# A two-layer decoder trunk with three token mixers: the matmuls of the mixers pinned to the program's order, with new tables for that order

## The chip, the cores and the metric

The kernel runs on one core of one Trainium2 chip. Its time is the time of one execution in microseconds on the device (us). "Before" is the kernel without the change, "after" is the kernel with it. TensorE is called PE in the profile, VectorE is DVE, ScalarE is ACT.

## The reference

The program computes two layers on 256 tokens of width 1024, in float32. Each layer is a half-step feed-forward network, a stage of three token mixers that run on one combined projection of x, a second half-step network, and an input embedding. The mixer stage is what the change touches.

```python
def token_mixing(x, w_in, ...):
    h = (x @ w_in).astype(jnp.float32)
    h_rw, h_gla, h_gdn, h_gate = _split(h, GROUP_SPLITS)
    o_rw = rwkv7_time_mix(h_rw, ...)
    o_gla = gla_mix(*_split(h_gla, GLA_SPLITS), ...)
    o_gdn = gated_deltanet_mix(*_split(h_gdn, GDN_SPLITS), ...)
    branches = jnp.stack([o_rw, o_gla, o_gdn], axis=2)
    proj = jnp.einsum('btnc,ncd->btnd', branches, w_branch)
    gates = jax.nn.sigmoid(h_gate).reshape(B, T, N_BRANCH, D_MODEL)
    merged = jnp.sum(gates * proj, axis=2)
    return merged.astype(x.dtype) @ w_o
```

Each mixer is a recurrence over time that the kernel computes in chunks: RWKV-7 with eight heads of 64, gated linear attention (GLA) with four heads, and gated DeltaNet (GDN) with four heads and a short causal convolution over its q, k and v.

## The kernel before

Every weight is split into a high and a low part so that a float32 product is three matmuls (x high by w high, x low by w high, x high by w low). A weight half arrives by DMA as `raw` (128x1024), ACT casts it to `hi`, and DVE subtracts to get `lo`. `ahead` issues this for the weights to come (four raw buffers, four pairs of hi and lo), and `unit` hands the next block out. PSUM is divided into three sets of banks: A with four, F with two and G with two; the table TAGS says which tile takes which set.

The mixer stage of a layer begins with the block fwa of the projection and ends with the output projection wo of `merge`. Four generators run in it. S (`stream`) computes the projection in blocks: a block `cb` is 48 matmuls of 128x256 into one bank (`col_block`), followed by what takes it out of the bank: `shift_mix` for RWKV (one ACT and one DVE instruction for each half; the tile is called c0, c512, ...), `conv` for GDN (one ACT and three DVE instructions for each half; c3888, c3376), a sigmoid-free copy `sg` to DRAM for the merge gates (`put`), or a copy. Later S projects the finished branches with `project` (tile `pj`). R (`rwkv`), D (`gdn`) and L (`gla`) are the chains of the three mixers. MIX lists the blocks in S's order, ORDER is a string that says which generator takes the next step, from one `yield` to the next.

Names that come up: in RWKV `pw` are the low-rank products of decay and `av`, `l2` the norm of kk (its operand `sq`, its row in the profile called l), `ls`, `bk` operands that are spread out for the Gram matrices `gram`, whose inverse is built in `rig`, `rigt`, `riab` (15 pairs of a multiply and a reduction on DVE), then `rix`, `rih`, and a recurrence of `rp`, `ru`, `rd`, `ry` over chunks; `bh`, `bl` are the high and low parts of the finished branch. In GDN `ab`, `gcol`, `grow`, `dd` are the decays, `un` the unit norms (operand `usq`), `gix`, `gih` the inverse, `gv`, `gd`, `go` the recurrence. In GLA `gk` is the forget gate, `lxb` its logarithm and running sum, `lw` the weighted q and k of a level, `lg` the Gram matrix of a level, `latt` the assembled attention.

A scheduler decides the order of each engine's instructions from the program's order, priorities and its own estimates; between instructions that depend on each other it adds semaphore waits. Each engine then runs its own list from front to back. Where `hold` is set, an instruction made through `Engine.__getattr__` is pinned, so that it keeps its place in the program's order on its engine. Before, only the Gram matmuls of RWKV are held so within the mixers.

Of the kernel before, what the change touches and what calls it, by code (L numbers as in the profile page):

```python
# [19 lines left out]
F32 = mybir.dt.float32  # L20
# [6 lines left out]
TAGS = {"ab": "A", "gcol": "A", "gih": "G", "gks": "G", "ktr": "F", "lc": "F", "lo": "A", "misc": "G", "pa": "G", "pg": "G", "pj0": "A", "pj1": "A", "pq": "A", "pw": "G", "rih": "G", "st0": "A", "st1": "G", "un": "F"}  # L27
# [3 lines left out]
P = 128  # L31
# [181 lines left out]
class Engine:  # L213


    def __init__(self, trunk, engine):
        self.trunk, self.engine = trunk, engine

    def __getattr__(self, name):
        f = getattr(self.engine, name)  # L220

        def call(*args, **kw):
            ins = f(*args, **kw)  # L223
            return self.trunk.pin(ins) if self.trunk.hold else ins

        return call


class Engines:
    def __init__(self, trunk, nc):  # L230
        self.tensor, self.vector, self.scalar = (Engine(trunk, e) for e in (nc.tensor, nc.vector, nc.scalar))
        self.gpsimd, self.sync = nc.gpsimd, nc.sync


class Trunk:
# [112 lines left out]
    def unit(self, *key):  # L348

        assert self.plan[self.used] == key, (self.plan[self.used], key)  # L350
        self.used += 1
        self.subtract()
        n = 1 if key[0] == "fmisc" else 2
        self.ahead(n - len(self.ready))
        parts = [self.ready.pop(0) for _ in range(n)]

        def part(a, n):
            q, o = divmod(a, 1024)
            return parts[q][0][:, o:o + n], parts[q][1][:, o:o + n]

        return part
# [308 lines left out]
    def mixers(self, i):  # L670

        self.got, self.branch, self.over = {}, {}, set()
        self.maker = {"b0": "R", "b1": "L", "b2": "D"}
        self.threads = {"S": self.stream(i), "R": self.rwkv(i), "D": self.gdn(i), "L": self.gla(i)}
        for name in ORDER + "RDLS":
            self.step(name)
        for name in "RDLS":
            while name not in self.over:
                self.step(name)

    def stream(self, i):
# [3 lines left out]
        ps = self.col_block(self.unit("fwa", i))  # L685
# [12 lines left out]
        ab = self.pt.tile([P, NT, 8], F32, tag="ab", name="ab", bufs=1)  # L698
        ps = self.ps("ab", "G")
        for t in range(NT):  # L700
            nc.tensor.transpose(ps[:, 8 * t:8 * t + 8], mx[64:72, t * P:t * P + P], self.ident[64:72, 64:72])
        A.copy(ab[:, :, 0:4], ps[:, :16].rearrange("p (t c) -> p t c", c=8)[:, :, 0:4])
        A.activation(ab[:, :, 4:8], ps[:, :16].rearrange("p (t c) -> p t c", c=8)[:, :, 4:8], AF.Sigmoid)
# [185 lines left out]
    def rwkv(self, i):  # L889
# [36 lines left out]
        A.activation(sq, kk, AF.Square)  # L926
        for q in range(2):
# [52 lines left out]
        for q in range(2):  # L980
            for c in range(2):
                m = slice(4 * c, 4 * c + 4)
                pss = [self.ps("gram").rearrange("p (n c) -> p n c", c=P) for _ in range(2)]
                self.hold = True
# [3 lines left out]
                self.hold = False  # L988
# [101 lines left out]
    def rwkv_out(self, t, y, bv, gl):  # L1090
# [4 lines left out]
        A.activation(rs, y, AF.Square)  # L1095
        ps = self.ps("rv")
# [53 lines left out]
    def unit_norms(self, xs):  # L1150
# [17 lines left out]
    def gdn(self, i):  # L1168
# [11 lines left out]
        ab = self.got["misc"][1]  # L1180
# [23 lines left out]
        pg = self.ps("gcol", "G")  # L1204
# [10 lines left out]
        for t in range(NT):  # L1215
            grow = self.ps("grow", "G").rearrange("p (h c) -> p h c", c=P)
# [14 lines left out]
        self.unit_norms([(k, 1.0), (q, float(P) ** -0.5)])  # L1231
# [7 lines left out]
        for t in range(NT):  # L1239
            pk, pq = self.ps("pk", "G"), self.ps("pq", "G")  # L1240
# [53 lines left out]
        for t in range(NT):  # L1294
# [12 lines left out]
            yield  # L1307
            if not t:
                vd = h3(self.s2("gvd"))
                V.tensor_tensor(out=vd, in0=vn, in1=self.head_bc(ec, P), op=ALU.mult)  # L1310
                pd = h3(self.ps("gd"))
# [3 lines left out]
                yield  # L1315
# [10 lines left out]
    def gla(self, i):  # L1326
# [83 lines left out]
        V.tensor_tensor(out=w4[:, :, 2:4], in0=w4[:, :, 2:4], in1=q4[:, :, 2:4], op=ALU.mult)  # L1410
        cross = self.s4("lcross").rearrange("p (a c) -> p a c", c=P)
# [24 lines left out]
    def project(self, i, b, h):  # L1436
# [39 lines left out]
        half(0)  # L1476
        half(1)
# [186 lines left out]
```

## Time and profile before

| | us |
|---|---|
| median of 3 runs | 1574.25 (1574.13 to 1577.86) |
| the profiled execution | 1568.71 |
| its span in the trace | 1566.9 |
| mean granted clock of TensorE | 0.981 |
| mixers of layer 0 | 217.0 to 539.5 |
| mixers of layer 1 | 995.7 to 1318.1 |

The page gives the busy time of every engine, the groups of instructions by line and tile, and the chain of work that ended last. The operations are recorded in a helper, so all of them have one line (L223 before, L224 after), and the groups are told apart by their tiles. A wait of an engine is put down to the instruction that released it. The granted clock is the share of full speed that TensorE was allowed.

### The profile page before, as it was taken

Reading aid. Unit: us, or ns where it says so; the run is one execution under the profiler, and the core shown is the slowest. Engines: PE = TensorE matmul, PEld = TensorE weight load, DVE = VectorE, ACT = ScalarE, POOL = GpSimd, SP = SyncE. Lnnn points to the kernel's source line nnn. Section 1 sums busy time; section 2 is a strip of 40 time slices with the busy share of each in tenths; the row PEclk is TensorE's granted clock in tenths of the full one; section 3 lists DMA queues with packets and bytes.
Section 4 is the critical chain, followed back from the end, with each engine's and each line's share of the span. In section 5 each row is a group of like instructions: output and inputs, shape, how many; then the busy total and the mean of one; then the engine's idle time right before and its main releaser. Section 6 shows DMA issues by size and latency. Waiting matters only on the chain. (4 is left out here: it accounts for less than half of the span.)

```text
span 1566.9 us, 27601 instructions
## 1 busy us (share of the span) xinstructions
PE 1494.9 (95%) x11280; PEld 1356.7 (87%) x11280; DVE 1058.5 (68%) x1597; ACT 873.3 (56%) x1229; POOL 49.1 (3%) x85
## 2 busy tenths in 40 slices
PE   8999999988998999999999999998989889999997
PEld 7999889887987989998789997897979879899986
DVE  5555757787975875556865557577789658745567
ACT  5544558856654554445654445587665555644453
POOL 0000000000002000000000000000000020000001
PEclk9999999989999999999999999999999999999999
DMA  7765655532424655656555666554425256656562
GB/s 257 264 215 189 216 190 161 169 127 80 151 84 168 233 184 177 223 189 216 177 180 192 216 189 194 195 170 153 136 75 156 82 200 219 188 170 222 189 217 81
DMA packets 79775, 277.96 MB, mean 177 GB/s; under 512 B 9376, under 2 KB 9760, under 8 KB 79648
## 3 DMA queue, kind: packets, MB, share of 16 engines
q1 hardware_dynamic: 75744, 262.76, 51.8%
q0 software_dynamic: 3616, 13.11, 2.2%
q8 instruction: 88, 1.44, 0.4%
q10 hardware_dynamic: 288, 0.33, 0.1%
q14 instruction: 39, 0.32, 0.1%
HBM read 264.63 MB, written 11.53 MB: 176 GB/s over the span
## 5 line engine op out<-in xcount | busy, mean ns | idle before, releaser
L223 DVE TENSOR_TENSOR lo<-raw,hi 128x1024 fp32r<-128x1024 f32 (+1 forms) x459 | 555.4, 1220 | 316.1 <-ACT hi L223 313.7
L223 ACT CAST hi<-raw 128x1024 fp32r<-128x1024 f32 (+1 forms) x459 | 474.9, 1047 | 430.1 <-PE h L223 144.1
L223 PE MATMUL h<-xh,hi 128*128 128x256 f32 x1088 | 306.2, 282 | 5.9 <-ACT hi L223 5.5
L223 PE MATMUL h<-xl,hi 128*128 128x256 f32 x1088 | 305.8, 281 | 0.8 <-DVE xl L223 0.8
L223 PE MATMUL h<-xh,lo 128*128 128x256 f32 x1088 | 305.4, 281 | 0.0
L223 PE MATMUL cb<-xh,hi 128*128 128x256 f32 x864 | 247.1, 286 | 14.4 <-DVE c L223 11.1
L223 PE MATMUL cb<-xl,hi 128*128 128x256 f32 x864 | 244.5, 283 | 0.0
L223 PE MATMUL cb<-xh,lo 128*128 128x256 f32 x864 | 243.4, 282 | 0.0
L223 PEld LDWEIGHTS h<-xh,hi 128*128 128x128 f32 x1088 | 204.9, 189 | 7.3 <-ACT hi L223 5.5
L223 PEld LDWEIGHTS h<-xh,lo 128*128 128x128 f32 x1088 | 208.6, 192 | 0.1
L223 PEld LDWEIGHTS h<-xl,hi 128*128 128x128 f32 x1088 | 205.1, 189 | 2.2 <-DVE xl L223 1.0
L223 PEld LDWEIGHTS cb<-xh,hi 128*128 128x128 f32 x864 | 164.7, 191 | 18.8 <-DVE c L223 11.3
L223 PEld LDWEIGHTS cb<-xl,hi 128*128 128x128 f32 x864 | 164.8, 191 | 2.4 <-issue 1.0
L223 PEld LDWEIGHTS cb<-xh,lo 128*128 128x128 f32 x864 | 164.7, 191 | 1.9 <-issue 1.0
L223 PE MATMUL y<-hi,gh 128*128 128x512 f32 x352 | 137.8, 391 | 0.0
L223 PE MATMUL y<-lo,gh 128*128 128x512 f32 x352 | 137.1, 389 | 0.0
L223 PE MATMUL y<-hi,gl 128*128 128x512 f32 x352 | 136.2, 390 | 0.3 <-DVE gl L223 0.3
L223 PE MATMUL tb<-hi,xl 128*128 128x512 f32 x224 | 87.6, 391 | 2.1 <-DVE xl L223 2.1
L223 PE MATMUL tb<-hi,xh 128*128 128x512 f32 x224 | 88.5, 395 | 0.0
L223 PE MATMUL tb<-lo,xh 128*128 128x512 f32 x224 | 88.0, 393 | 0.0
L223 PEld LDWEIGHTS y<-hi,gl 128*128 128x128 f32 x352 | 66.1, 188 | 14.7 <-DVE gl L223 0.8
L223 PEld LDWEIGHTS y<-lo,gh 128*128 128x128 f32 x352 | 66.1, 188 | 12.2
(354 smaller groups left out, 2264.0 us busy)
## 6 DMA issues: line engine op xcount, KB each, us to landing
raw<-in_ws_dram SPq DMA_DIRECT2D x457, 512.0 KB, 4.4
gb<-in_ln_dram SPq DMA_DIRECT2D x16, 512.0 KB, 6.1
gd<-sg SPq DMA_DIRECT2D x32, 256.0 KB, 4.2
sgate<-gd POOLq DMA_DIRECT2D x12, 512.0 KB, 5.8
xd<-x POOLq DMA_DIRECT2D x4, 512.0 KB, 5.8
x<-xd POOLq DMA_DIRECT2D x4, 512.0 KB, 9.0
sw<-in_sw_dram SPq DMA_DIRECT2D x2, 768.0 KB, 8.7
xt<-in_xt_dram SPq DMA_DIRECT2D x4, 256.0 KB, 5.4
```

The costliest lines, as they stand in the source:

```text
L223: ins = f(*args, **kw)
```

## The change

In the mixers PE's instructions are pinned to the program's order, by a flag `eager` that holds for `tensor` alone; DVE and ACT are still ordered by the scheduler. So that the program's order is one to follow, a block yields after its first 24 matmuls, and the chains get further yields so that one step holds one burst of matmuls; the Gram matmuls of a GLA level are issued a step later than their operands; the transposes of `ab` go from the stream to `gdn`. MIX, ORDER and TAGS are new. `unit` asks for two more weight halves ahead while `eager` is set. The work is the same: the same matmuls, DVE and ACT instructions, except for four more ACT_TABLE_LOADs in the whole program.

```diff
-TAGS = {"ab": "A", "gcol": "A", "gih": "G", "gks": "G", "ktr": "F", "lc": "F", "lo": "A", "misc": "G", "pa": "G", "pg": "G", "pj0": "A", "pj1": "A", "pq": "A", "pw": "G", "rih": "G", "st0": "A", "st1": "G", "un": "F"}
+TAGS = {"gk": "G", "lc": "G", "lg": "G", "lo": "G", "misc": "F", "pg": "G", "pj0": "F", "pj1": "F", "st0": "F", "st1": "F",
+        "tp": "G"}
...
-MIX = (C_R, C_K, C_DK, C_LV, (0, 0), C_V, C_LQ, (0, 1), C_DQ, (2, 0), (1, 1), C_DV, (2, 1), (1, 0), ("w", 0, 0),
...
+MIX = (C_K, C_R, (2, 0), C_LQ, (2, 1), C_DK, C_DQ, (1, 0), C_V, C_LV, (1, 1), C_DV, ("w", 1, 0), ("w", 1, 1), (0, 0), (0, 1),
+       ("w", 0, 0), ("w", 0, 1), ("w", 2, 0), ("w", 2, 1))
+ORDER = ("SSSRRSRDLSSDSRSSRSRSRSRSRSSRSRSRSSLSRSLSRSLSRLSRSRLSRSRLSRSRSRDSSSRSRSRDLSSRRSRDLRSRDLRSDLSRDLRS"
...
-            return self.trunk.pin(ins) if self.trunk.hold else ins
+            return self.trunk.pin(ins) if self.trunk.hold or self.first and self.trunk.eager else ins
...
-        self.tensor, self.vector, self.scalar = (Engine(trunk, e) for e in (nc.tensor, nc.vector, nc.scalar))
+        self.tensor, self.vector, self.scalar = (
+            Engine(trunk, e, e is nc.tensor) for e in (nc.tensor, nc.vector, nc.scalar))
...
+        if self.eager:
+            self.ahead(2 - len(self.ready))
...
-    def tok_unit(self, pss, unit, k0, start, stop, x=None):
+    def tok_unit(self, pss, unit, k0, start, stop, x=None, qs=range(2)):
...
             for k in range(8):
                 self.col_mm(ps[:, c * T:c * T + T], unit, k, c)
+            if not c:
+                yield
         return ps
...
+        self.eager = True
         for name in ORDER + "RDLS":
...
+        self.eager = False
...
         A.activation(sq, kk, AF.Square)
+        yield
         for q in range(2):
             ps = self.ps("l2")
...
-                self.hold = True
                 for n in range(4):
                     for e, (r, o) in enumerate(halves):
                         self.mm(pss[e][:, n], bk[q][r, 4 * c + n], ls[e][q][r, 4 * c + n])
-                self.hold = False
...
+        mx = self.got["misc"][1]
+        ab = self.pt.tile([P, NT, 8], F32, tag="ab", name="ab", bufs=1)
+        ps = self.ps("ab")
...
         for n, s in enumerate(LEVELS):
+            if n:
+                grams(*last)
...
-            grams(w, w, 1 + n, s)
+            last = w, w, 1 + n, s
             yield
+        grams(*last)
+        yield
         grams(k, q, 0, 0)
-        yield
```

Three places show how the lists of ACT and DVE come out. The first is ACT's list at the start of layer 0's mixers, where `ab` (GDN's decays) and `lxb` (GLA's gate, taken out of the bank gk) are made. Before, from the end of the tile misc:

```order
L223 COPY gl_2286<-mx 16x256
L223 CAST hi<-raw 128x1024 x2
L223 ACTIVATE c_2494<-cb,om 128x256
L223 COPY ab<-ab 128x2x4
L223 ACTIVATE ab<-ab 128x2x4
L223 ACTIVATE c_2494<-cb,om 128x256
L223 ACT_TABLE_LOAD
L223 ACTIVATE e<-e 128x8
L223 CAST hi<-raw 128x1024 x2
```

and, a hundred rows later, gk's turn:

```order
L223 CAST hi<-raw 128x1024 x2
L223 ACTIVATE sg<-cb 128x512
L223 ACTIVATE c_2363<-c_2363,cv 128x256 x2
L223 ACTIVATE lxb<-gk,cv 128x256 x2
L223 COPY uz<-ru 64x256 x2
```

After, from the copies out of pw on:

```order
L224 ACTIVATE sg<-pw,cv 128x256
L224 ACTIVATE av<-pw,cv 128x256
L224 ACT_TABLE_LOAD
L224 ACTIVATE sg<-sg 128x1024
L224 COPY ab<-ab 128x2x4
L224 ACT_TABLE_LOAD
L224 ACTIVATE ab<-ab 128x2x4
L224 ACTIVATE lxb<-gk,cv 128x256
L224 ACT_TABLE_LOAD
L224 ACTIVATE e<-e 128x8
L224 ACTIVATE lxb<-gk,cv 128x256
L224 CAST hi<-raw 128x1024
```

`ab` and both `lxb` copies now follow directly on pw, with three table loads between them. The second is ACT's list from the spread operands `ls` of RWKV to the copy of a merge gate's block (`sg`) out of its bank. Before:

```order
L223 COPY ls01_2960<-sg_2296 64x8x64
L223 COPY ls11_2962<-sg_2296 64x8x64
L223 ACT_TABLE_LOAD
L223 ACTIVATE c3888_2651<-c3888_2651 128x1024
L223 CAST hi_3089<-raw_3087 128x1024
L223 COPY lv_2891<-st1_2818 128x512
L223 ACT_TABLE_LOAD
L223 ACTIVATE sq_2722<-cs_2357 128x1024
L223 CAST hi_3148<-raw_3146 128x1024
L223 ACTIVATE cs_2357<-cs_2357 128x1024
L223 CAST hi_3154<-raw_3152 128x1024
L223 ACTIVATE sg_2956<-cb_2907 128x512
```

After:

```order
L224 COPY ls10_2773<-sg_2345 64x8x64
L224 COPY ls01_2772<-sg_2345 64x8x64
L224 COPY ls11_2774<-sg_2345 64x8x64
L224 CAST hi_2736<-raw_2734 128x1024
L224 CAST hi_2742<-raw_2740 128x1024
L224 ACTIVATE c0_2583<-cb_2667,om_783 128x256
L224 ACTIVATE sq_2577<-cs_2401 128x1024
L224 CAST hi_2816<-raw_2814 128x1024
L224 ACTIVATE cs_2401<-cs_2401 128x1024
L224 ACTIVATE c0_2583<-cb_2667,om_783 128x256
L224 CAST hi_2822<-raw_2820 128x1024
L224 ACTIVATE sg_2802<-cb_2746 128x512
```

The copy `sg` of block cb_2746 stands behind the rest of the chain (its steps on `sq` and `av` are just ahead of the rows shown), the ls copies and four casts; PE's next block, cb_2826, waits for it. The third is DVE's list at the convolution of the GDN key (c3888). Before, the DVE steps on block cb_2664 stand in a run, and the Gram steps follow some 30 rows later:

```order
L223 TENSOR_TENSOR lo_2822<-raw_2819,hi_2821 128x1024
L223 TENSOR_TENSOR lo_2828<-raw_2825,hi_2827 128x1024
L223 SCALAR_TENSOR_TENSOR c3888_2651<-cb_2664,cv_775,c3888_2651 128x255
L223 SCALAR_TENSOR_TENSOR c3888_2651<-cb_2664,cv_775,c3888_2651 128x254
L223 SCALAR_TENSOR_TENSOR c3888_2651<-cb_2664,cv_775,c3888_2651 128x253
L223 SCALAR_TENSOR_TENSOR c3888_2651<-cb_2664,cv_775,c3888_2651 128x255
L223 SCALAR_TENSOR_TENSOR c3888_2651<-cb_2664,cv_775,c3888_2651 128x254
L223 TENSOR_TENSOR lo_2858<-raw_2855,hi_2857 128x1024
L223 SCALAR_TENSOR_TENSOR c3888_2651<-cb_2664,cv_775,c3888_2651 128x253
L223 TENSOR_TENSOR lo_2864<-raw_2861,hi_2863 128x1024
```

After, a stretch of the steps on blocks cb_3247 and cb_3377:

```order
L224 SCALAR_TENSOR_TENSOR c3888_3234<-cb_3247,cv_775,c3888_3234 128x254
L224 COPY_PREDICATED latt_3013<-masks_79,lg_3406 128x32x8
L224 COPY_PREDICATED latt_3013<-masks_79,lg_3407 128x32x8
L224 STREAM_TRANSPOSE rigt_3553<-rig_3457 128x512
L224 SCALAR_TENSOR_TENSOR c3888_3234<-cb_3247,cv_775,c3888_3234 128x253
L224 TENSOR_TENSOR lo_3466<-raw_3463,hi_3465 128x1024
L224 TENSOR_TENSOR riab_3555<-rigt_3553 128x256
L224 TENSOR_TENSOR lo_3472<-raw_3469,hi_3471 128x1024
L224 SCALAR_TENSOR_TENSOR c3888_3234<-cb_3377,cv_775,c3888_3234 128x255
L224 SCALAR_TENSOR_TENSOR c3888_3234<-cb_3247,cv_775,c3888_3234 128x255
L224 TENSOR_TENSOR rigt_3553<-riab_3555 128x1
L224 SCALAR_TENSOR_TENSOR c3888_3234<-cb_3377,cv_775,c3888_3234 128x254
```

The steps that empty these two banks are spread among the Gram steps, the GLA levels, the transposes and the first steps of the inverse.

More of the change, by code (lines that the diff above doesn't have):

```diff
@@ L54 @@
     0, 128, 256, 384, 512, 544, 672, 800, 802, 804, 932)
-MIX = (C_R, C_K, C_DK, C_LV, (0, 0), C_V, C_LQ, (0, 1), C_DQ, (2, 0), (1, 1), C_DV, (2, 1), (1, 0), ("w", 0, 0),
-       ("w", 1, 1), ("w", 0, 1), ("w", 1, 0), ("w", 2, 0), ("w", 2, 1))
-ORDER = ("RRSRSSSDSSRSRRSSSRRRRRRRRRRSSRSRRRSDRRRRRSRSRDRRRRRRRRDRDSDRLDRRDRDLRDDSDSSSLDLDRLRDRRRDRDDRRRDLRLDD"
-         "SDDDDSDLLSDDDLLRDLSDLLRRLLDSSDSDSLLSSSSDSLDS")
+MIX = (C_K, C_R, (2, 0), C_LQ, (2, 1), C_DK, C_DQ, (1, 0), C_V, C_LV, (1, 1), C_DV, ("w", 1, 0), ("w", 1, 1), (0, 0), (0, 1),
+       ("w", 0, 0), ("w", 0, 1), ("w", 2, 0), ("w", 2, 1))
+ORDER = ("SSSRRSRDLSSDSRSSRSRSRSRSRSSRSRSRSSLSRSLSRSLSRLSRSRLSRSRLSRSRSRDSSSRSRSRDLSSRRSRDLRSRDLRSDLSRDLRS"
+         "DSDLLSRDLRSDLLLSRDLSRDSRDLSRDSRDRSRDSRDSRDRRSRDSRDRRSDSRSRDRSRDDSRDSRDDSRDSRDRDSDSDSSSS")
 LEVELS = (64, 32, 16, 8, 4, 2, 1)
@@ L213, with __init__ @@
 class Engine:
-    def __init__(self, trunk, engine):
-        self.trunk, self.engine = trunk, engine
+    def __init__(self, trunk, engine, first):
+        self.trunk, self.engine, self.first = trunk, engine, first
     def __getattr__(self, name):
@@ L366, in mm3 @@
         self.mm(out, ll, rh, False, stop)
-    def tok_unit(self, pss, unit, k0, start, stop, x=None):
+    def tok_unit(self, pss, unit, k0, start, stop, x=None, qs=range(2)):
         xh, xl = x or (self.xh, self.xl)
-        for q in range(2):
+        for q in qs:
             for t in range(NT):
@@ L679, in mixers @@
                 self.step(name)
+        self.eager = False
     def stream(self, i):
@@ L684, in stream @@
         A = nc.scalar
-        ps = self.col_block(self.unit("fwa", i))
+        ps = yield from self.col_block(self.unit("fwa", i))
         wa = self.pt.tile([P, T], F32, tag="wa", name="wa", bufs=1)
@@ L697, in stream @@
         self.shift_mix(mx, ps[:, :T], 14)
[L698 to L703, printed above, removed]
         nc.gpsimd.memset(gl[:, 1:], 0.0)
@@ L706, in stream @@
         A.copy(gl[32:48, 2], mx[32:48])
-        self.got["misc"] = gl, ab
+        self.got["misc"] = gl, mx
         yield
@@ L711, in stream @@
                 yield "b%d" % item[1]
-                self.project(i, *item[1:])
+                yield from self.project(i, *item[1:])
                 if item != MIX[-1]:
@@ L717, in stream @@
                 for u in range(2):
-                    ps = self.col_block(self.unit("fcol", i, C_MG + item[0] * D + item[1] * 512 + 256 * u))
+                    ps = yield from self.col_block(self.unit("fcol", i, C_MG + item[0] * D + item[1] * 512 + 256 * u))
                     self.put(ps, d, u, AF.Copy)
@@ L725, in stream @@
                 for u in range(2):
-                    self.tok_unit(pss, self.unit("tok", i, item, u), 4 * u, u == 0, u == 1)
-                    if u == 0:
-                        yield
+                    un = self.unit("tok", i, item, u)
+                    for q in range(2):
+                        self.tok_unit(pss, un, 4 * u, u == 0, u == 1, qs=(q,))
+                        if (u, q) != (1, 1):
+                            yield
                 vt = self.s4("lv").rearrange("p (t c) -> p t c", t=2)
@@ L736, in stream @@
                 q, k = qk[:, :512], qk[:, 512:]
-                A.activation(q, self.col_block(self.unit("fcol", i, C_LQ)), AF.Identity, scale=0.125)
+                ps = yield from self.col_block(self.unit("fcol", i, C_LQ))
+                A.activation(q, ps, AF.Identity, scale=0.125)
                 yield
-                A.copy(k, self.col_block(self.unit("fcol", i, C_LK)))
+                ps = yield from self.col_block(self.unit("fcol", i, C_LK))
+                A.copy(k, ps)
                 self.got[item] = q, k
@@ L744, in stream @@
                 for u in range(2):
-                    ps = self.col_block(self.unit("fcol", i, item + 256 * u))
+                    ps = yield from self.col_block(self.unit("fcol", i, item + 256 * u))
                     for c in range(2):
@@ L1095, in rwkv_out @@
         A.activation(rs, y, AF.Square)
+        yield
         ps = self.ps("rv")
@@ L1157, in unit_norms @@
             sqs.append(sq)
+        yield
         for sq in sqs:
             for q in range(2):
-                ps = self.ps("un", "G")
+                ps = self.ps("un")
                 s = slice(q * 512, q * 512 + 512)
@@ L1179, in gdn @@
         yield "misc"
-        ab = self.got["misc"][1]
+        mx = self.got["misc"][1]
+        ab = self.pt.tile([P, NT, 8], F32, tag="ab", name="ab", bufs=1)
+        ps = self.ps("ab")
+        for t in range(NT):
+            nc.tensor.transpose(ps[:, 8 * t:8 * t + 8], mx[64:72, t * P:t * P + P], self.ident[64:72, 64:72])
+        A.copy(ab[:, :, 0:4], ps[:, :16].rearrange("p (t c) -> p t c", c=8)[:, :, 0:4])
+        A.activation(ab[:, :, 4:8], ps[:, :16].rearrange("p (t c) -> p t c", c=8)[:, :, 4:8], AF.Sigmoid)
         e, s, s2, q, x = (small(n) for n in ("e", "s", "s2", "q", "x"))
@@ L1203, in gdn @@
         tri = kc[:, K_INCL:K_INCL + P]
-        pg = self.ps("gcol", "G")
+        pg = self.ps("gcol")
         self.mm(pg[:, :8], tri, x.rearrange("p t h -> p (t h)"))
@@ L1215, in gdn @@
         for t in range(NT):
-            grow = self.ps("grow", "G").rearrange("p (h c) -> p h c", c=P)
+            grow = self.ps("grow").rearrange("p (h c) -> p h c", c=P)
             for h in range(4):
@@ L1230, in gdn @@
         k, q = self.got[C_DK], self.got[C_DQ]
-        self.unit_norms([(k, 1.0), (q, float(P) ** -0.5)])
+        yield from self.unit_norms([(k, 1.0), (q, float(P) ** -0.5)])
         yield
@@ L1239, in gdn @@
         for t in range(NT):
-            pk, pq = self.ps("pk", "G"), self.ps("pq", "G")
+            pk, pq = self.ps("pk"), self.ps("pq")
             for h in range(4):
@@ L1310, in gdn @@
                 V.tensor_tensor(out=vd, in0=vn, in1=self.head_bc(ec, P), op=ALU.mult)
+            yield
+            if not t:
                 pd = h3(self.ps("gd"))
@@ L1314, in gdn @@
                 A.copy(st, pd)
-                yield
             ops = self.ps("go")
@@ L1374, in grams @@
                     "p (a b s) -> p a b s", a=4, s=out.shape[3]))
-        lw = None
+        lw = last = None
         for n, s in enumerate(LEVELS):
+            if n:
+                grams(*last)
             v5 = lambda ap: ap.rearrange("p (m f s) -> p m f s", f=2, s=s)
@@ L1392, in gla @@
             V.tensor_tensor(out=v5(w)[:, :, 1], in0=v5(w)[:, :, 1], in1=v5(q)[:, :, 1], op=ALU.mult)
-            grams(w, w, 1 + n, s)
+            last = w, w, 1 + n, s
             yield
+        grams(*last)
+        yield
         grams(k, q, 0, 0)
-        yield
         w = lw[:, 512:]
@@ L1410, in gla @@
         V.tensor_tensor(out=w4[:, :, 2:4], in0=w4[:, :, 2:4], in1=q4[:, :, 2:4], op=ALU.mult)
+        yield
         cross = self.s4("lcross").rearrange("p (a c) -> p a c", c=P)
@@ L1476, in project @@
         half(0)
+        yield
         half(1)
```

1 line of the change is left out of this document (removed).

## The prediction

> **What bounds the kernel now.** I read the page's first part, then the windows of the two mixer stages, the table of what TensorE (PE) waits for there, and last the clock.
>
> ```profile
> PE 1494.9 (95%) x11280; PEld 1356.7 (87%) x11280; DVE 1058.5 (68%) x1597; ACT 873.3 (56%) x1229; POOL 49.1 (3%) x85
> 217.00:539.50 322.50, 299.17 (x2842) 276.52 (x2841) 242.50 (x435) 208.19 (x304) 13.58 (x25) 0.95 0.45 147
> 995.70:1318.10 322.40, 296.79 (x2841) 274.40 (x2840) 241.90 (x434) 207.65 (x304) 12.72 (x23) 0.96 0.45 148
> ```
>
> The kernel is PE's: 95% busy. The windows run from the first cb matmul of a layer's mixers to its first wo matmul, and are the only stages that the change touches. The columns are length, then busy time of PE, weight loads, DVE, ACT, POOL, then the granted clock. PE idles 322.50 - 299.17 = 23.3 us in layer 0 and 322.40 - 296.79 = 25.6 us in layer 1. Those 49 us, and the clock of 0.95, are all that a better order can win. They are few waits (the first five of layer 0, and the one row of layer 1 that differs most):
>
> ```profile
> PE pj L223 <- ACT bh L223: 6.0, 1, 6.0
> PE cb L223 <- DVE c L223: 5.4, 1, 5.4
> PE un L223 <- ACT usq L223: 4.0, 1, 4.0
> PE gtf L223 <- ACT gt L223: 1.9, 1, 1.9
> PE bkt L223 <- DVE ls L223: 1.3, 1, 1.3
> PE cb L223 <- ACT hi L223: 1.6, 1, 1.6
> ```
>
> The clock falls behind such waits, here after the pair c and usq and after a broken stretch at 437:
>
> ```profile
> 312.50:322.70 10.20, 4.68 (x21) 4.59 (x22) 9.49 (x29) 1.18 (x3) 0.00 (x0) 0.50 0.13 45
> 437.00:442.20 5.20, 2.43 (x30) 1.74 (x26) 2.05 (x5) 4.97 (x7) 0.00 (x0) 1.00 0.00 0
> 442.20:449.00 6.80, 6.12 (x92) 5.43 (x92) 5.66 (x14) 4.24 (x10) 0.00 (x0) 0.50 0.01 2
> ```
>
> At half clock half of the busy time is loss: 4.68 / 2 = 2.3 us and 6.12 / 2 = 3.1 us, 2.7 us in the mean. Each mixer stage has four such stretches (about 10.8 us).
>
> **What the change does, and the durations for it.** The same matmuls, casts and vector operations run before and after. Nothing is removed; only their order, the PSUM banks and, with four more table loads in the program (4 x 1.28 = 5 us of ACT time), ACT's switching differ. So the sum is one of waits: PE's list is now fixed, and at each point I add up what the ACT and DVE lists put ahead of the result that PE wants, and take off the matmuls that PE has to do meanwhile. Mean ns of one, from the groups of layer 0's mixers:
>
> ```profile
> L223 ACT CAST hi<-raw 128x1024 fp32r<-128x1024 f32 x72 | 74.4, 1049 | 58.9 <-PE cb L223 37.4 <-PE pj L223 14.9 <-issue 4.7
> L223 ACT ACT_TABLE_LOAD x21 | 26.9, 1283 | 1.2 <-DVE c L223 0.8
> L223 ACT ACTIVATE sg<-cb 128x512 f32<-128x512 f32 x12 | 7.1, 592 | 0.0
> L223 ACT ACTIVATE c<-cb,om 128x256 f32<-128x256 f32 x12 | 5.5, 474 | 4.0 <-DVE c L223 3.9
> L223 ACT COPY ls<-sg 64x512 f32<-64x512 f32 x4 | 2.5, 620 | 0.0
> L223 ACT ACTIVATE sq<-av,om,cv 128x256 f32<-128x256 f32 x4 | 2.2, 593 | 0.0
> L223 ACT ACTIVATE dd<-grow,gcol 128x128 f32<-128x128 f32 x8 | 2.2, 392 | 0.0
> L223 ACT ACTIVATE sq<-l,eps 128x512 f32<-128x512 f32 x2 | 1.4, 688 | 0.5 <-PE l L223 0.5
> L223 ACT ACTIVATE sg<-sg 128x1024 f32<-128x1024 f32 x1 | 1.1, 1062 | 0.0
> L223 DVE TENSOR_TENSOR lo<-raw,hi 128x1024 fp32r<-128x1024 f32 x73 | 88.3, 1220 | 23.6 <-ACT hi L223 22.6 <-PE cb L223 0.3
> L223 DVE SCALAR_TENSOR_TENSOR c<-cb,cv,c 128x255 f32<-128x255 f32 (+2 forms) x48 | 22.7, 477 | 2.5 <-ACT c L223 1.9
> L223 DVE COPY_PREDICATED latt<-masks,lg 128x256 f32<-128x256 uint8 (+1 forms) x16 | 7.9, 553 | 2.2 <-PE lg L223 2.2
> L223 DVE TENSOR_TENSOR lw<-lw,lqk 128x256 f32<-128x256 f32 x16 | 6.1, 421 | 0.0
> L223 DVE TENSOR_TENSOR ls<-gram,kc 64x512 f32<-64x512 f32 x8 | 5.5, 688 | 0.1
> L223 DVE TENSOR_TENSOR rig<-gram,kc 32x256 f32<-32x256 f32 x8 | 4.7, 590 | 0.1
> L223 DVE TENSOR_TENSOR rigt<-riab 128x1 f32<-128x1 f32 (+14 forms) x15 | 4.6, 306 | 0.5
> L223 DVE TENSOR_REDUCE riab<-rigt 128x1 f32<-128x1 f32 (+14 forms) x15 | 3.6, 238 | 0.4
> L223 DVE STREAM_TRANSPOSE rigt<-rig 128x512 f32<-128x512 f32 x3 | 2.1, 705 | 1.6 <-ACT rit L223 1.6
> L223 DVE TENSOR_TENSOR rig<-riab,kc 128x512 f32<-128x512 f32 x2 | 1.7, 868 | 0.0
> L223 DVE SCALAR_TENSOR_TENSOR q<-q,s 128x8 f32<-128x8 f32 x8 | 1.3, 161 | 0.1
> ```
>
> PE's own pace is the distance of two starts in the timeline; 77 matmuls of cb lie from the first row to the last:
>
> ```profile
> 246.99 0.28 PE L223 MATMUL cb<-xl,hi 128*128 128x256 f32 x1
> 255.73 0.28 PE L223 MATMUL cb<-xh,hi 128*128 128x256 f32 x1
> ```
>
> (255.73 - 246.99) / 77 = 0.1135 us, so a half block of 24 gives 2.7 us of cover and a block of 48 gives 5.45 us. Where a shape has no row of its own here I use the row of the same width.
>
> **The sum for one layer**, in PE's new order. Each term is a wait of PE, with its ends:
>
> 1. pw behind misc. PE has nothing between them: cast (1.05), mx and two wz copies at 0.47 = 2.5. Taken 2.5 (0 to 2.5).
> 2. gk's second bank. The lists have ab and gk right behind pw: table load 1.28, sg 1.06, two tiny ab copies 0.3, table load 1.28, lxb 0.47 = 4.4. Taken 4.0 (2.1, if the first load and half the sg lie earlier, to 4.4).
> 3. gcol. On DVE two lo 2.44, two c 0.95, two 512-wide and two 256-wide lxb steps at 0.69 = 2.8, 16 tiny steps at 0.161 = 2.6: 8.8; one ACT table load and exponential among them 1.4; less 48 cb and gk, 5.7: 4.5. Taken 4.5 (2 to 6).
> 4. l2 wants sq. Behind grow ACT has dd 8 x 0.39, a table load, four hi 4.2, six 256-wide steps 2.8, one 512-wide 0.7, two 1024-wide 2.1 = 14.2; cover 72 cb and grow, 9.2; the first dd run beside grow. Taken 4.6 (3 to 5.1).
> 5. cb behind the first gate block. Its bank is freed by sg, in front of which ACT now has three c 1.4, two table loads 2.6, two sq<-l 1.4, three 1024-wide 3.2, four sq<-av 2.4, four ls 2.5, four hi 4.2; with sg 0.6 that is 18.3. Cover l2 and 96 cb, 11.8: 6.5. A kk step of DVE (1.2) may add to it. Taken 6.5 (5.7 to 7.6).
> 6. The k half of lqk waits for the next sg: four bk and ls pairs at 0.62, two hi, sg: 7.6 - 5.5 = 2.1 (0 to 2.1).
> 7. The convolutions. Their banks are freed by DVE, 12 c steps for C_DK (5.7) and nine of C_DQ (4.3). Before, these stood ahead of the grams; now they stand among and behind seven lo 8.6, eight lw 3.4, six gram and ls steps 2.6, four rig 2.4, four latt 1.7 (these at their narrower 0.43), three transposes 2.1, the whole inverse 15 x 0.306 + 15 x 0.238 = 8.2, and two 0.87 rig: 40.7 in all. PE has 19.3 of its own from there to cb of the third block. 40.7 - 19.3 = 21.4 as upper end; 14.6 if what DVE does before the first grams lies beside earlier waits. Taken 18, as two waits.
> 8. pj of branch R behind bh. The chain rsq, ro, tp, bh is as it was: 6.0 (to 8.9 with two more half-width steps in the queue).
> 9. The rest: the smaller waits of the tables (about 4) remain, and lc, rd, ktr and sgate each meet one of about 1. Taken 8 (4 to 17).
>
> Sum: 2.5 + 4.0 + 4.5 + 4.6 + 6.5 + 2.1 + 18 + 6.0 + 8 = 56.2 us (37 to 75). Old c, un and gtf waits are thereby counted as gone. Added idle: 56.2 - 23.3 = 32.9 and 56.2 - 25.6 = 30.6, together 63.5 us. Clock: seven waits of 4 us or more stand in place of four slow stretches, 3 x 2.7 x 2 = 16.2. The profiled execution's 1568.7 becomes 1648.4. The median lies 1574.25 - 1568.7 = 5.5 above that execution, so **1654 us**.
>
> The slow stretch at 442.20 followed a window in which PE was idle more than half of the time, in pieces. By the Trainium skill ("TensorE: Matmul & The Clock Gate", "Why this matters for your kernels") only gaps of more than about 3 us drop the clock; terms 1 and 6 then cost no clock. By this trace's row they could cost a stretch each, another 2 x 2 x 2.7 = 11 us. I leave them out of the sum either way.
>
> **Rivals.**
> - *DVE has run ahead.* PE's waits 2 to 6 (21.7 us) give DVE time to empty its list, and term 7 shrinks to 5, with one slow stretch less: 1654 - 2 x (13 + 2.7) = 1623; with terms 1 to 3 at their lower ends 1600. For it: DVE idles 80 us of the stage (322.5 - 242.5). Against it: the grams, inverse and conv steps of term 7 all need banks that PE fills only there. Case 1580 to 1620.
> - *The late bursts wait too.* Some 25 short bursts of the chains (ru, rp, ry, rd, gv, go and so on) stand pinned between half blocks, each with 2.7 us of cover for one round of ACT and DVE. If each is 1 us late: 1654 + 2 x 25 = 1704. For it: nothing can now pass a late burst. Against: late in the stage DVE has the lightest load. Case 1690 to 1730.
> - *Faster.* Chains start early and the late waits of before go, while the early ones stay small. With terms 1 to 6 at 8 (only ACT's surplus of work over PE's), term 7 at 5, bh 6, rest 4, idle is 23 us, as now, and only two slow stretches remain: 1574.25 - 0.3 - 2.6 - 4 x 2.7 = 1560.5. It decides at idle and clock loss together under 23.3 + 10.8 = 34 us a layer. Against: the row of sg stands behind 18 us of ACT work in its own list, and PE may not pass it.
> - *Nothing.* The pin has no effect, or every added wait is paid by one that goes: 1574. The order of PE does change, so little is left for it.
>
> **How the numbers follow.** Forecast case (1620 to 1690) 0.51, mild (1580 to 1620) 0.20, heavy (1690 to 1730) 0.14, faster 0.11, nothing 0.04. The range 1582 to 1712 leaves out faster, nothing and the end of heavy, about 0.2. Differences within 0.3%, 4.7 us, can't be told from no change; so faster 0.11, same 0.04, slower 0.85.
>
> **What would show it.** Mixer windows some 40 us longer each at 0.90 to 0.93 clock, all else unmoved. In the table of waits: gcol from DVE near 4.5, l2 from ACT sq near 4.6, cb from ACT sg near 8 to 9, cb from DVE c near 18, un and gtf gone. I am wrong if PE's idle stays under 34 us a layer, if cb from c is under 8, or if the bulk of waits stands in the second half of a mixer stage.

## The result: 1635.0 us, 3.8% slower

The changed kernel takes 1635.0 us in the median of four runs (1634.42 to 1635.29), the kernel before 1574.19 in the runs beside it; the ratio is 1.0384 (95% interval 1.0368 to 1.0399). The profiled execution took 1634.8 us. Its windows over the two mixer stages, cut at the same matmuls as before, from the first cb to the first wo (length, busy PE, weight loads, DVE, ACT, POOL, clock):

```profile
218.70:569.10 350.40, 301.48 (x2841) 279.92 (x2840) 241.35 (x434) 210.17 (x304) 12.85 (x24) 0.93 0.42 135
1031.10:1381.60 350.50, 300.68 (x2841) 279.23 (x2840) 241.73 (x434) 210.12 (x304) 11.99 (x22) 0.93 0.41 135
```

Each stage is 28 us longer than before (322.5 and 322.4). DVE and ACT do the same work in it as before; PE's idle time rose from 23.3 to 350.40 - 301.48 = 48.9 us and from 25.6 to 49.8 us. The rest of the program went from 217.0 + 456.2 + 248.9 = 922.1 us to 932.3. That execution of before was 5.5 us under its own median, and two other kernels whose code outside the mixers is that of before (e2_pin_only and e13_cv_a, below) take 1723.0 - 398.2 - 397.0 = 927.8 and 1572.0 - 322.8 - 321.4 = 927.8 us there. So some 6 of the 10 us are likely the one short execution of before; the others, among them waits of 1 to 2 us at gT and wo, weren't followed further.

Where the 48.9 us lie is shown by the table of PE's waits in layer 0's mixers (us in total, times, longest; its first nine rows):

```profile
PE cb L224 <- ACT c L224: 8.8, 1, 8.8
PE pj L224 <- ACT bh L224: 7.7, 1, 7.7
PE cb L224 <- DVE c L224: 6.3, 1, 6.3
PE cb L224 <- ACT sg L224: 4.7, 1, 4.7
PE l L224 <- ACT sq L224: 3.6, 1, 3.6
PE gcol L224 <- issue: 3.4, 1, 3.4
PE gk L224 <- ACT lxb L224: 3.3, 1, 3.3
PE pw L224 <- issue: 2.7, 1, 2.7
PE rd L224 <- DVE vs L224: 2.6, 3, 1.5
```

These are the places that the prediction named, nearly one for one. The old waits for c behind the grams, at un and at gtf are gone. Where the profile shows no semaphore for a wait it says issue; in layer 1 gcol's stands under DVE x (3.3 us), as forecast. Otherwise layer 1 has the same list within 0.6 us of each, with ACT's ritt (5.7) in the place of DVE's c, and one wait of 1.3 us for hi more. What stands behind such a wait can be read in the timeline of ACT ahead of sg, the copy that frees a bank of the gate block (start, duration, what, and in brackets the idle time before it):

```profile
270.89 1.28 ACT L224 ACT_TABLE_LOAD   x1
272.19 1.27 ACT L224 ACTIVATE sq<-l,eps 128x512 f32<-128x512 f32 x2
273.47 1.28 ACT L224 ACT_TABLE_LOAD   x1
274.76 1.06 ACT L224 ACTIVATE sq<-sq 128x1024 f32<-128x1024 f32 x1
277.12 2.08 ACT L224 ACTIVATE sq<-av,om,cv 128x256 f32<-128x256 f32 x4 [1.29 <-DVE kk L224]
279.11 2.51 ACT L224 COPY ls<-sg 64x512 f32<-64x512 f32 x4
281.64 2.00 ACT L224 CAST hi<-raw 128x1024 fp32r<-128x1024 f32 x2
...
288.05 0.60 ACT L224 ACTIVATE sg<-cb 128x512 f32<-128x512 f32 x1
```

PE has nothing to do from 284.04 to 288.7 us; ACT works from 270.9 on with one pause of 1.29 us, in its own order, and comes to sg last: the copy stands far back in its list.

### The profile page after: what moved, and what is told of

Its sections match the earlier page's. It is cut to its first block, busy times and chain, and to the rows that moved or that the text cites. A ratio compares the mean times of both kernels' runs of the same rounds, so it can differ in the third digit from the quotient of the medians.

```text
span 1633.1 us, 27571 instructions
## 1 busy us (share of the span) xinstructions
PE 1504.2 (92%) x11280; PEld 1367.1 (84%) x11280; DVE 1060.9 (65%) x1597; ACT 881.4 (54%) x1233; POOL 50.4 (3%) x85
## 4 chain that ended last, share of the span: by engine, by line
PE 68%; DVE 12%; ACT 10%; DMA 5%; issue 3%; POOL 1%; SPq 0%; POOLq 0%; DVEq 0%; ACTq 0%
PE h L224 23%; PE cb L224 15%; PE y L224 11%; DMA raw<-in_ws_dram 5%; DVE lo L224 4%; PE pj L224 4%; PE tb L224 4%; ACT hi L224 3%; ACT L224 2%; PE wo L224 2%; PE st L224 1%; DVE z L224 1%; DVE c L224 1%; ACT sq L224 1%; PE lg L224 1%
## 5 line engine op out<-in xcount | busy, mean ns | idle before, releaser
L224 PE MATMUL cb<-xh,hi 128*128 128x256 f32 x864 | 258.5, 299 | 40.8 <-ACT c L224 17.6
L224 PE MATMUL cb<-xh,lo 128*128 128x256 f32 x864 | 248.5, 288 | 1.9 <-DVE lo L224 1.9
L224 PE MATMUL cb<-xl,hi 128*128 128x256 f32 x864 | 248.7, 288 | 0.0
L224 PEld LDWEIGHTS cb<-xh,hi 128*128 128x128 f32 x864 | 172.4, 199 | 46.1 <-ACT c L224 17.9
L224 PEld LDWEIGHTS cb<-xl,hi 128*128 128x128 f32 x864 | 172.5, 200 | 2.1 <-issue 1.7
L224 PEld LDWEIGHTS cb<-xh,lo 128*128 128x128 f32 x864 | 171.7, 199 | 2.3 <-DVE lo L224 2.3
```

## The experiments

Times are medians. Each ratio is to the kernel before, run beside it: 1574.19 us for after, 1576.15 for e1, e2, e4 and e5, 1575.6 for e7, e8, e9 and e11, 1575.99 for the last four. Idle is PE's in layer 0's mixers, in us.

| label | edit | us | ratio (95%) | idle |
|---|---|---|---|---|
| after | the change | 1635.0 | 1.0384 (1.0368 to 1.0399) | 48.9 |
| e1_unpinned | after, PE not pinned | 1591.1 | 1.0109 (1.0072 to 1.0146) | 26.0 |
| e2_pin_only | before, PE pinned | 1722.4 | 1.0929 (1.0873 to 1.0985) | 78.6 |
| e4_pin_all | after, DVE and ACT pinned too | 1691.3 | 1.0732 (1.0688 to 1.0775) | 64.9 |
| e5_pin_pe_dve | after, DVE pinned too | 1669.8 | 1.0595 (1.0550 to 1.0640) | 55.5 |
| e7_moved | after, early bursts moved | 1619.7 | 1.0273 (1.0237 to 1.0308) | 42.2 |
| e8_conv_a | after, convolutions in set A | 1625.7 | 1.0316 (1.0290 to 1.0341) | 43.6 |
| e9_old_tags | e1 with the old sets | 1624.4 | 1.0307 (1.0285 to 1.0329) | 41.5 |
| e11_free_late | e1, decays late | 1588.6 | 1.0080 (1.0057 to 1.0102) | 26.5 |
| e13_cv_a | before, C_V in set A | 1579.8 | 1.0021 (1.0004 to 1.0037) | 24.8 |
| e14_conv_free | e11, convolutions in set A | 1585.7 | 1.0062 (1.0039 to 1.0085) | 31.4 |
| e12b_levels_conv | e14, levels late | 1583.7 | 1.0044 (1.0025 to 1.0064) | 25.9 |
| e15_pinned_mended | e7 + e8 + end of ORDER | 1592.8 | 1.0107 (1.0087 to 1.0127) | 35.6 |

### The pin or the tables?

```diff
-            return self.trunk.pin(ins) if self.trunk.hold or self.first and self.trunk.eager else ins
+            return self.trunk.pin(ins) if self.trunk.hold else ins
```

> The changed kernel with its new MIX, ORDER, TAGS and yields, but nothing pinned in the mixers: the scheduler places PE's instructions too. Theory A (the waits come from the new order of blocks and chains, which brings work of ACT and DVE in front of results that PE wants; the pin adds little): its PE list differs from the changed kernel's at few places; gcol and grow move behind 45 more matmuls, so the gcol wait (3.4 us) goes and some single us late in the stage; the waits for sq, sg and c stay. 2 x (3.4 + 1.5 to 3) less, 1618 to 1628 us. Theory B (the pin is what costs): PE fills its gaps, idle per mixer stage back at some 24 us, 1565 to 1585 us.

Neither. 1591.1 us lies between the two: of the change's 60 us or so the pin holds 44 and the new tables, with everything else, 15. Theory A was too sure of the few places at which the two PE lists differ early on. PE's waits without the pin, layer 0:

```profile
PE cb L224 <- DVE c L224: 7.6, 3, 5.0
PE lg L224 <- DVE latt L224: 5.1, 2, 2.7
...
PE pj L224 <- ACT bh L224: 2.7, 1, 2.7
```

Without the pin the scheduler saves a little almost everywhere: sg's wait is gone, gcol's 3.4 became 0.5, the convolutions' 15.1 us became 10.4 (c 5.0, latt 5.1 and 0.3), and pj's 7.7 became 2.7. From its middle on (379.2 to 541.5 us) the stage has 162.30 - 157.58 = 4.7 us of idle time where the pinned one (393.9 to 569.1) has 175.20 - 160.02 = 15.2.

The other way round, the pin alone on the old program (the lines of the change that set `first` and `eager` and pin by them, put into the kernel before; not the one that asks for more weights ahead):

> The kernel before, with its own MIX, ORDER, TAGS and yields, and PE pinned to the program's order in the mixers. Theory A (an order of work is good or bad by what covers each wait; a pin takes the cover from an order that was not written for it): the old program order has chain steps right behind each other (gram sets, rix, rih, un, levels of lg, rp and ru) with no block between them, so some 12 to 20 steps per layer wait 2 to 4 us each, 30 to 60 us more a layer, 1630 to 1700 us. Theory B (the pin itself costs about 60 us in any order): near 1635. Theory C (the pin is harmless): 1574.

1722.4 us, beyond even theory A's range: the old program order was never one to run in order. The 55 us of idle time that layer 0 gains (78.6 against 23.3) are within theory A's 30 to 60; what lies beyond it is the clock, 0.88 in the stage where before had 0.95.

```profile
PE lg L223 <- DVE lw L223: 10.3, 2, 6.6
PE ktr L223 <- ACT c L223: 7.8, 1, 7.8
PE un L223 <- ACT usq L223: 7.5, 2, 6.6
```

So the yields, tables and half blocks of the change do what they are made for: with the pin they are 87 us better than the old order. They are only not as good as the scheduler's choice of PE's order.

### Are the lists of DVE and ACT at fault?

```diff
-            return self.trunk.pin(ins) if self.trunk.hold or self.first and self.trunk.eager else ins
+            return self.trunk.pin(ins) if self.trunk.hold or self.trunk.eager else ins
```

> The changed kernel with DVE and ACT pinned to the program's order as well in the mixers. Theory A (waits come from what stands ahead in the DVE and ACT lists): the convolution steps now stand in runs of six on DVE directly behind their blocks, ahead of the inverse, so the waits for c (8.8 and 6.3) shrink to 1 to 4 in all; the wait for sg stays within 1 us of 4.7, since the list of ACT in front of it keeps 16 us of work; with one or two slow clock stretches less, 12 to 18 us less per layer, if nothing else is late: 1600 to 1612. Theory B (the scheduler's lists of ACT and DVE are better than the program's, whose chain steps that wait for PE then hold up the casts of the weights behind them): new waits for hi and lo at the start of blocks, 1640 to 1700.

For the second, ACT is left free (`Engine(trunk, e, e is not nc.scalar)`):

> The changed kernel with PE and DVE pinned and ACT left to the scheduler. Theory A: the waits for c go as with all three pinned (DVE's list is what held the banks), those of ACT (sq, lxb, sg) stay as in the changed kernel: 1602 to 1615. If it is ACT's list that holds the banks of the convolution, the waits for c stay over 10 us a layer and the time is 1630 to 1640.

The first came out in theory B's range, 1691.3 us; the second, 1669.8 us, is above both of its ranges. In the kernel with all three pinned, of PE's waits and then of those of ACT and DVE:

```profile
PE cb L224 <- ACT hi L224: 12.3, 4, 5.2
PE cb L224 <- DVE lo L224: 8.2, 6, 5.0
...
PE cb L224 <- DVE c L224: 4.5, 1, 4.5
...
ACT lw L224 <- DVE lw L224: 33.5, 8, 12.1
ACT c L224 <- DVE c L224: 29.5, 14, 10.4
...
DVE lo L224 <- ACT hi L224: 62.2, 25, 9.7
```

The wait for c falls from 15.1 to 4.5 us, near theory A's 1 to 4, but the blocks of PE wait for their weights instead: 12.3 + 8.2 us. Theory B saw the casts behind chain steps that wait for PE; the rows show them behind steps that wait for DVE above all (lw 33.5 and c 29.5 us), and DVE's subtractions wait 62.2 us for the casts in turn. With DVE pinned and ACT free, PE waits 4.2 us for c and 12.1 us for `lo`, so ACT's list was not what held the convolutions' banks. A list in program order is worse for these two engines than the scheduler's, by 35 us (DVE) and 56 us (both).

### Does the place of a burst make the wait?

```diff
-ORDER = ("SSSRRSRDLSSDSRSSRSRS...
+ORDER = ("SSSRRSRDSLSSRSDSSSRR...
```

> The changed kernel, PE pinned, with seven early steps of ORDER moved so that PE's pinned list stands about as the scheduler puts it without the pin: gk behind the second half of its block, gcol and grow one block later, l2 one block later. Theory A (what a pin costs is the place that the program gives a burst, not the pin): by the new ACT list sq is ahead of dd, so the wait at l2 goes (3.6 to under 1), gcol's goes (3.4 to under 1), sg's falls from 4.7 to 1 to 2, gk's stays near 3; with three slow clock stretches less a layer 10 to 18 us less in each, 1600 to 1615. Theory B (with PE pinned the scheduler's lists of ACT and DVE are worse wherever the bursts stand): the same idle at other places, 1625 to 1640.

```profile
PE cb L224 <- ACT c L224: 7.9, 1, 7.9
...
PE cb L224 <- ACT ritt L224: 7.0, 1, 7.0
PE gk L224 <- ACT lxb L224: 4.3, 1, 4.3
```

1619.7 us, 15 less than the changed kernel, just above theory A's range and under theory B's. The wait at gcol (3.4) and at l2 (3.6) are out of the table, sg's is 0.9 in place of 4.7; gk's grew to 4.3, and the convolutions' 14.9 us (7.9 and 7.0) stay. The pin itself is as it was.

### Banks, or DVE's own work?

```diff
-                    ps = yield from self.col_block(self.unit("fcol", i, item + 256 * u))
+                    ps = yield from self.col_block(self.unit("fcol", i, item + 256 * u), "A" if item in (C_DK, C_DQ) else "F")
```

> The changed kernel with the four blocks of the q and k convolutions in set A (four banks) instead of F (two banks), nothing else. Theory A (PE waits there because two banks come free late): the next blocks find banks in F, the 8.8 and 6.3 us waits for c go and at most 5 us come back at un or rix, with 17 us less at half clock: 2 x (10 to 17) less, 1600 to 1615. Theory B (DVE is behind by its own work, 40 us for 19 us of PE, and the bank is only where PE meets it): the wait moves to the grams, levels or un behind it and the time stays at 1625 to 1638.

```profile
PE rix L224 <- ACT rit L224: 9.3, 1, 9.3
...
PE cb L224 <- ACT bkt L224: 1.6, 1, 1.6
```

Theory B by the time, 1625.7 us, though the wait came back at rix, a place that theory A had named. The waits for c are gone, but 9.3 us stand at rix, which needs the inverse that DVE is still working on, and 1.6 behind bkt: 10.9 in place of 15.1. So for some 70% of the wait the bank was only where PE met DVE's list; the other 4.2 us went with the banks.

The same on the kernel before, whose one long wait for c lies on the blocks of C_V:

> The kernel before with the two blocks of C_V in PSUM set A instead of F. Before, PE waits 5.4 us for DVE's c behind the grams and the clock is low for 10.2 us after it. If that wait is for a bank of F, it goes and some of it comes back at the next thing that DVE is late with: 2 x (3 to 8) less, 1558 to 1570. If DVE is simply behind there, within 3 us of before, 1572 to 1578.

Ratio 1.0021 (1.0004 to 1.0037), no gain. The 5.4 us at cb are gone and PE waits 6.9 us at the first gram for ACT's bk. But this run doesn't tell whether DVE was simply behind, because PE isn't pinned here and the scheduler changed its order with the banks: between l2 and the first gram PE now has 96 matmuls of cb, where before had 145, and comes to that gram at 289.8 us. ACT's bk lets it start at 296.7 us, at nearly the same time as before (295.9). The new wait is earlier than the old one and on another engine:

```profile
PE gram L223 <- ACT bk L223: 6.9, 1, 6.9
```

The PSUM sets as a whole, put back in the unpinned kernel (the TAGS line of before, with grow and pk in G as they were):

> As the unpinned kernel (1591), with the PSUM sets of before for the tiles that the change moved. If the new TAGS cost part of the 15 to 17 us that the unpinned kernel is over the old one, 1575 to 1586; if MIX and ORDER cost them, 1587 to 1600, with the waits for c, latt and sq at their places.

1624.4 us, against both sides of the expectation: with the new order the new sets, and what the scheduler makes of them, are worth 33 us. With the old ones ktr waits 10.0 us and cb 11.7:

```profile
PE cb L223 <- DVE c L223: 11.7, 2, 6.5
PE ktr L223 <- DVE c L223: 10.0, 1, 10.0
```

### A version that beats both?

Three tries without the pin. First the decays later in ORDER (its steps 3 to 28, counted from 0):

```diff
-RRSRDLSSDSRSSRSRSRSRSRSSRS
+SRRRSSSRSSRSRSRSRSDRSLSRSD
```

> As the unpinned kernel, with pw behind half a block more and the decays of GDN and GLA (ab, gk, gcol, grow) some five blocks later in ORDER. Theory A (the early part is bound by ACT's and DVE's work, which the new ORDER brings forward): the waits pw 2.5, gk 0.9, l2 2.9 and c 0.9 and 1.7 go, and one slow stretch a layer: 1570 to 1580. Rival (the same work only meets the grams and convolutions later): their waits grow by as much, 1588 to 1600.

Then the convolutions in set A (the edit of e8_conv_a), and with that GLA's levels later (steps 45 to 94):

```diff
-LSRSRLSRSRLSRSRSRDSSSRSRSRDLSSRRSRDLRSRDLRSDLSRDLR
+SRSRSRSRSRLSRSRDSSSRSRSRLDSSRRSRLDRSRDRLSDLSLRDLRL
```

> As the unpinned kernel with late decays (1589), with the q and k convolutions' blocks in set A. If the waits for latt (2.4 and 2.7) and c (3.9) hang on the two banks, they go with the 10.2 us at half clock behind them, 1566 to 1576, level with or under the kernel before; if as in the pinned kernel two thirds of the wait come back at rix, 1580 to 1588.

> As the one with late decays and convolutions in set A, and with six steps of GLA's levels 10 to 20 steps later in ORDER. If DVE's load between the first gram and rix (levels, grams, inverse, convolutions together) is what is left of the early waits, 5 to 10 us better than without it; if it only moves the levels onto the rih part, the same within 4 us.

1588.6, 1585.7 and 1583.7 us, against 1576 for the kernel before: each is on its rival's side, and none beats it; the steps of 2 to 3 us between the three are within their intervals. In the second, the waits for latt at these places (6.2 us in the first) are gone, and one of 9.5 us is at st for DVE's c:

```profile
PE st L224 <- DVE c L224: 9.5, 1, 9.5
PE cb L224 <- DVE c L224: 5.8, 1, 5.8
```

### All pinned mends together

The edits of e7_moved and e8_conv_a, and the end of ORDER (steps 163 to 174), so that pg, rv and go come before the last half block in front of pj:

```diff
-SRDDSRDSRDRD
+RSRDDDRSDSDR
```

> PE pinned, with three things mended together: the early bursts moved (measured 15 us), the convolutions in set A (9.5 us), and at the end of the mixers pg, rv and go ahead of the last half block before pj of branch R, so that 24 cb and go cover the chain to bh. Theory A (each pinned wait is the place of one burst): the wait at pj falls from 7.7 to 3 to 4 with 3.4 us less at half clock, the others add up: 1620 - 9.5 - 10 to 18, 1588 to 1603. Theory B (gains of single mends overlap, a wait that goes in one place comes back in another): 1605 to 1620.

```profile
PE rix L224 <- ACT rit L224: 9.2, 1, 9.2
...
PE pj L224 <- ACT bh L224: 4.3, 1, 4.3
```

1592.8 us, within theory A's range: 42 us less than the changed kernel, of which 15 and 9 belong to the first two edits by their own runs. The third wasn't run alone; the wait at pj fell from 7.7 to 4.3, which with the clock (0.95 and 0.96 in the two stages, 0.93 after) is where the rest must lie. So with PE pinned all the way, some moved bursts and four blocks in other banks win back 42 us, about as much as the 44 that lifting the pin wins. Most of what the pin costs here is the place at which the tables put some bursts. That all of it is, isn't shown: the unpinned kernel with late decays and the convolutions in set A (e14_conv_free) is 7 us faster still.

## Why the prediction held, and where its sizes were off

The forecast was 1654 us in 1582 to 1712; the direction, the mechanism and the places were right, the time was 19 us too long. None of its signs of being wrong came: idle is 48.9 us in layer 0, the convolutions' wait 15.1, and 15.2 of the 48.9 lie in the second half. But a stage grew by 28 us, not by 40. Its terms against the waits of the two layers:

| term | forecast | layer 0 | layer 1 |
|---|---|---|---|
| 1 pw | 2.5 | 2.7 | 2.7 |
| 2 gk | 4.0 | 3.3 | 3.2 |
| 3 gcol | 4.5 | 3.4 | 3.3 |
| 4 l2 | 4.6 | 3.6 | 3.5 |
| 5 sg | 6.5 | 4.7 | 5.0 |
| 6 second sg | 2.1 | 0 | 0.3 |
| 7 convolutions | 18 | 15.1 | 14.5 |
| 8 pj behind bh | 6.0 | 7.7 | 7.7 |
| 9 the rest | 8 | 8.4 | 9.6 |
| idle in the stage | 56.2 | 48.9 | 49.8 |

**Terms 2 to 5 and 7** are each 0.7 to 3 us too high. The durations account for little of it: in the timeline above four sq<-av take 2.08 us, not 4 x 0.593 = 2.37, and two casts 2.00, not 2.10, but four ls take 2.51, where the sum had 2.5. What terms 3 and 5 had wrong is PE's cover. The sum took the clock and the waits as two separate losses; but a half-clock stretch behind one wait makes the matmuls ahead of the next one last longer, and so covers more of that next wait. The cb matmuls alone between gk and gcol, and between l2 and sg's wait:

```profile
242.48:250.43 7.95, 7.94 (x48) 7.65 (x48) 0.47 (x1) 0.47 (x1) 0.71 0.18 55
270.98:284.04 13.06, 13.06 (x96) 12.34 (x96) 0.41 (x1) 0.47 (x1) 0.87 0.12 41
```

The 48 took 7.95 us in place of 5.45, the 96 took 13.06 in place of 10.9. The other side came out longer than the sum had it: gcol's operand was there 7.95 + 3.4 = 11.3 us after gk (10.2 in the sum), and the sg copy ended 19.1 us after l2 began (18.3 in the sum; the kk step of DVE that "may add" held ACT for 1.29 of them). **Term 7** stood at the lower end (14.6) of its bounds, not near the upper; there too the 24 cb behind its first wait took 5.4 us at half clock in place of 2.7, ahead of its second.

**Term 8** went the other way. "The chain is as it was" missed ACT's list: ahead of rsq a gate's activation with a table load on each side now stands in it. Before (first row) the gate's activation came behind rsq, and one load stood ahead:

```profile
494.23 0.69 ACT L223 ACTIVATE rsq<-rv,eps 128x512 f32<-128x512 f32 x1
...
530.71 1.28 ACT L224 ACT_TABLE_LOAD   x1
532.01 1.06 ACT L224 ACTIVATE sgate<-sgate 128x1024 f32<-128x1024 f32 x1
533.08 1.28 ACT L224 ACT_TABLE_LOAD   x1
534.38 0.69 ACT L224 ACTIVATE rsq<-rv,eps 128x512 f32<-128x512 f32 x1
...
539.72 0.62 ACT L224 CAST bh<-ro 128x512 fp32r<-128x512 f32 x1 [2.71 <-DVE ro L224]
```

The load and the activation that came in front take 1.28 + 1.06 = 2.3 us, against the 1.7 by which the wait grew.

**The clock** was counted as three more slow stretches a layer, 8.1 us. There are eight in layer 0, one more than forecast, but several are short or hold idle time:

```profile
240.20:247.00 6.80, 5.18 (x22) 5.00 (x23) 2.96 (x14) 4.99 (x8) 0.00 (x0) 0.50 0.00 0
...
346.00:356.30 10.30, 5.19 (x24) 5.19 (x24) 9.79 (x33) 3.22 (x4) 0.00 (x0) 0.50 0.34 103
...
sum 47.70, PE 34.65 PEld 33.66 DVE 28.76 ACT 21.89 POOL 0.00; mean PE 4.33 PEld 4.21 DVE 3.60 ACT 2.74 POOL 0.00
```

Half of 34.65 us is 17.3 us lost, against half of 22.29 (the four stretches of before) = 11.1: 6.2 us more in layer 0, and by the same reckoning 7.1 in layer 1 (31.87 and 17.66 busy). The two short waits that were left out of the sum, with 11 us as their price, cost no clock at pw, and the other did not occur.

**A term that was missing.** Take the slow loss off the busy time and PE's work in layer 0 is 301.48 - 17.3 = 284.2 us, where it was 299.17 - 11.1 = 288.0; in layer 1 284.7 and 288.0. The sum took them as equal. The new order by itself doesn't bring this: by the same reckoning it has 287.8 us in layer 0 without the pin (e1_unpinned), and the old order has 283.1 with it (e2_pin_only). So it comes with the pin. Part of it is the reckoning, which takes half of the slow busy time as lost: in the traces of after and before two cb matmuls start 0.226 and 0.224 us apart at half clock and 0.118 at full clock, 1.9 times and not 2, and two of ry (before) 1.5 times. That a burst pinned in one piece is also cheaper than one whose matmuls stand among those of a block would fit the rest, but no run here takes it apart.

Together: idle 7.3 + 6.4 us less than forecast, clock 1.9 + 1.0 less, matmuls 3.8 + 3.2 less, so the mixers are 24 us shorter than the sum; the rest of the program was 10 longer than in the execution that the sum started from. And the 5.5 us between the profiled execution and the median, added at the end, don't exist for this kernel (1634.8 and 1635.0). The last two cancel part of the first: that the forecast came within 19 us and not 24 is luck.

The rivals: that DVE has run ahead held in part (term 7 at its lower end), but 15.1 us is far from the 5 that it would have left; its 1600 also isn't what its terms give, since terms 1 to 3 at their lower ends take 6.9 us a layer off 1623, which is 1609. The late bursts did not wait in any number: rd 2.6, gih 1.3 and ktr 1.3 us are all of it. The faster case did not come: idle and clock loss together are 48.9 + 17.3 = 66 us in layer 0, not under 34. The reason given against it, the sg row in ACT's list, held PE for 4.7 us of that.

## What to carry to other kernels

Pinning one engine's list turns every other engine's list into a deadline: count, for each burst, what the other engines have in front of its operand and compare it with the matmuls ahead of it; here that sum named every large wait to within 40%, the small second sg wait apart. Count the cover at the clock that PE will have: matmuls at half clock cover nearly twice as long, so what the clock costs and what the waits cost aren't two separate sums. A bank that comes free late can be only where the wait shows: with more banks for the convolutions some 70% of it stood one step further on, at the result that the busy engine was still working on. And an order written by hand for one engine doesn't carry over to the others: pinning DVE and ACT too put the weights' casts behind chain steps of ACT that wait for DVE, and DVE's subtractions behind the casts.

## What the runs showed of the hardware

The granted clock fell behind short gaps too. Before 486 us PE waits once for 1.50 us, and 3.4 us at half clock follow; the wait of 2.7 us at pw (228.6 us), on the other hand, was followed by full speed up to 240 us. What tells the two apart is a fixed grid. The slow stretches are 3.4, 6.8 or 10.2 us long, whole multiples of 3.41, and within each trace they all begin on one grid of that step. On it the short gap falls into one window, and the longer one is split between two:

```profile
226.56:229.97 3.41, 2.03 (x18) 1.83 (x17) 0.82 (x2) 3.01 (x4) 0.00 (x0) 1.00 0.11 46
229.97:233.38 3.41, 2.12 (x5) 1.06 (x6) 1.88 (x3) 2.77 (x9) 0.00 (x0) 1.00 0.27 67
...
482.57:485.98 3.41, 1.78 (x32) 1.43 (x31) 3.03 (x6) 0.94 (x3) 0.00 (x0) 1.00 0.70 195
485.98:489.39 3.41, 3.41 (x18) 3.41 (x17) 0.65 (x2) 0.81 (x2) 0.00 (x0) 0.50 0.32 118
```

Laid on this grid, from 20 us on, the traces of all fourteen kernels here show half clock behind each of the 185 full-speed windows in which PE was busy for under 0.42 of the time, behind 5 of some 5800 with over 0.60, and both outcomes in between (1.78 us of 3.41 is 0.52, the two windows at pw have 0.60 and 0.62). The same holds for a stretch that the prediction put down to the wait for c: at half clock from 312.33 us on, it begins ahead of that wait (313.2 to 318.6 us), behind a window with 1.81 us busy in pieces. The Trainium skill ("TensorE: Matmul & The Clock Gate", "What's actually happening") tells of a free-running window of about 3.4 us, which agrees with these lengths; its advice to have no gaps over about 3 us ("Why this matters for your kernels") fits the gap at pw and would have let the one of 1.50 us pass, and there the measured one decides.
